# Values by seven block products of half size, 512 columns a pass

## The chip, the core and the metric

One core of a Trainium2 chip runs the whole program. Five engines work from queues of their own, in order: TensorE (PE, matmuls), VectorE (DVE), ScalarE (ACT), GpSimd (POOL) and SyncE (SP, which here only issues DMA transfers). They wait for each other by semaphores. Matmuls read SBUF and add into eight banks of PSUM; DVE and ACT read the banks out. ACT and POOL can issue transfers too. The metric is the device time of one execution in microseconds, as the median of the runs.

## The reference

A decoder trunk of two layers over 1024 tokens of width 1024, in float32. Layer 0 mixes tokens by pooling and has a gated FFN. Then keys and values for three attention branches are projected from the residual stream; layer 1 attends to them with its own queries and has an FFN. Each sub-layer is normalised and modulated by vectors computed from a conditioning vector `c`.

```python
kv_shift, kv_scale = jnp.split(cond @ kv_ada_w + kv_ada_b, 2, axis=-1)
hkv = _modulate(_rmsnorm(x, kv_norm_g), kv_shift, kv_scale)
kv = (hkv @ w_kv).reshape(b, s, 2, N_BRANCHES, N_HEADS, HEAD_DIM)
y = _dilated_attention(h, kv, attn_w_q[j], attn_w_o[j], slopes)
```

The change concerns the value half of `hkv @ w_kv`: (1024 tokens x 1024) times (1024 x 3072).

## The kernel before, in words

**Three passes for a product.** Float32 operands are split in a high part (`hi`, rounded by ACT) and a remainder (`lo`, by DVE). A product of two 128-row blocks is three matmul passes: hi x hi, hi x lo, lo x hi. `wprep` and `split` (L105 to L114) make the parts of a weight block of 128x1024; `wraw`, `whi` and `wlo` have 3, 5 and 5 buffers.

**Seven products in place of eight.** The FFN's up projection and the queries already use a seven-product scheme (class `Pair`, L404): a 2x2 block product is formed from sums of weight blocks (`s1` to `s4`, on DVE) and sums of activation blocks (`T1` to `T4`, class `Ops`), with results added in the banks pX and pY. There the weights are the stationary operand and 512 token columns move. A query pair has 7 products of 12 passes, or 5 where two were done ahead (pairs 0 to 7 of 12).

**Values, L985 to L1018.** Normalised and modulated activations (`hx`, `hkx`, then `h` in `hk`) are the stationary operand; weights move, 256 columns a pass. 12 column groups of 256, 2 token halves, 4 blocks of 128 tokens, 8 blocks of the inner dimension, 3 passes each. ACT reads a bank (`vt`) and stores 512 KB at a time to `vd` in DRAM.

**Conditioning vectors beside it, L316 to L332.** `ada_run` computes vectors 8 to 11 in the value stage: a row block `araw` of 128x1024 is loaded by SP, multiplied by the broadcast `condr` on POOL and summed in four pieces on ACT. Vectors 8 to 10 are needed at the attention's output projection and the norm after it, 11 at the second FFN's down projection.

**What sets the order.** Outside of blocks marked `manual_schedule` a scheduler with a timing model puts every engine's instructions in an order and gives tiles their buffers. The query and value stages were such code. Within a marked block the named engines follow the order in which the code was written. Attention follows, with PE in written order: key projections (from `hk`, line L1108) fill the gaps, and slabs of q and v are loaded two units ahead.

The small buffers of the query stage are the tag `t2` (5 of 128x512): the two intermediate results `qh` of a pair, the saved results `p` and `qc` that are loaded back for pairs 0 to 7.

## Time and profile before

| | us |
|---|---|
| median of 3 runs (2821.94 to 2826.0) | 2823.73 |
| the profiled execution | 2824.13 |
| its span, first to last instruction | 2822.4 |
| PE busy | 2712.8 (96%) |
| DVE busy | 1795.5 (64%) |
| ACT busy | 1197.4 (42%) |
| POOL busy | 552.8 (20%) |

The query stage ends at about 1200 us, value passes run from 1190.3 to 1474.9 us, key passes from there to 1990 us. A matmul's printed duration covers its way through the array, in which others run beside it: the cost of one in a stream is the stretch divided by the count.

### The profile page before, as it was taken

How to read it: one execution, taken by the hardware profiler on the slowest of the kernel's cores; microseconds unless marked ns; L12 is line 12 of the kernel's file. 1: busy time of each engine (PE TensorE's matmuls, PEld its weight loads, DVE VectorE, ACT ScalarE, POOL GpSimd, SP SyncE). 2: the span in 40 equal slices, each digit the busy share in tenths (PEclk: the TensorE clock that was granted, in tenths of full speed). 3: DMA queues.
4: the chain of work that ended last, by engine and by line, in shares of the span. 5: the costliest groups of instructions: out<-in, count | busy, mean ns of one | idle time of the engine just before them, and what ended most of it. 6: DMA issues, size and time to landing. Idle time of an engine off the chain costs nothing.

```text
span 2822.4 us, 38016 instructions
## 1 busy us (share of the span) xinstructions
PE 2712.8 (96%) x14220; PEld 2233.7 (79%) x14220; DVE 1795.5 (64%) x3215; ACT 1197.4 (42%) x2599; POOL 552.8 (20%) x454
## 2 busy tenths in 40 slices
PE   8988999999999999999999999999889999999997
PEld 4767888888778788899997777777667888888886
DVE  6897898776755687521114555656758986666554
ACT  4534545545541433334425444445345444443112
POOL 2476001102540300014410222222152000000001
PEclk9998999999999999999999999999999999999998
DMA  7424443334743355355532333334334432226221
GB/s 293 165 91 162 161 160 127 108 94 152 281 171 97 127 201 193 126 190 188 190 130 69 99 100 100 107 100 145 111 98 157 141 118 88 75 90 216 90 75 60
DMA packets 148825, 384.29 MB, mean 136 GB/s; under 512 B 15536, under 2 KB 53408, under 8 KB 148640
## 3 DMA queue, kind: packets, MB, share of 16 engines
q1 hardware_dynamic: 109872, 292.90, 31.2%
q10 hardware_dynamic: 26496, 50.34, 4.8%
q0 software_dynamic: 12272, 38.62, 4.2%
q8 instruction: 112, 1.84, 0.3%
q14 instruction: 73, 0.60, 0.1%
HBM read 295.75 MB, written 86.05 MB: 135 GB/s over the span
## 4 chain that ended last, share of the span: by engine, by line
PE 70%; DVE 8%; DMA 8%; issue 5%; POOL 2%; ACT 2%; SPq 0%; ACTq 0%; DVEq 0%; POOLq 0%
PE pX L414 8%; PE pX L415 8%; PE pX L416 8%; PE dps L340 5%; PE dps L341 5%; PE dps L342 5%; PE pY L414 3%; PE pY L416 3%; PE pY L415 3%; PE vps L1014 3%; PE vps L1013 3%; PE vps L1012 3%; PE kps L340 2%; DMA araw<-in_ada_t_dram 2%; PE kps L342 2%
## 5 line engine op out<-in xcount | busy, mean ns | idle before, releaser
L107 DVE TENSOR_TENSOR wlo<-wraw,whi 128x1024 fp32r<-128x1024 f32 x164 | 229.8, 1409 | 306.9 <-ACT whi L106 304.2
L340 PE MATMUL dps<-slab,whi 128*128 128x512 f32 x832 | 329.9, 398 | 12.1 <-DVE x L376 8.2
L341 PE MATMUL dps<-slab,whi 128*128 128x512 f32 x832 | 327.5, 394 | 1.1 <-DVE slab L107 1.1
L342 PE MATMUL dps<-slab,wlo 128*128 128x512 f32 x832 | 324.3, 393 | 3.5 <-DVE wlo L107 3.5
L323 POOL TENSOR_TENSOR araw<-araw,condr 128x1024 f32<-128x1024 f32 x72 | 184.7, 2570 | 601.8 <-ACT condr L894 277.2
L106 ACT ACTIVATE whi<-wraw 128x1024 fp32r<-128x1024 f32 x164 | 170.1, 1053 | 281.8 <-PE dps L341 144.5
L376 DVE SCALAR_TENSOR_TENSOR x<-dps,mods,x 128x512 f32<-128x512 f32 x280 | 202.3, 745 | 136.4 <-PE dps L342 133.7
L1185 ACT ACTIVATE ss<-ss,ngm 128x128 f32<-128x128 f32 (+1 forms) x384 | 168.0, 439 | 196.8 <-DVE ngm L1182 183.7
L1013 PE MATMUL vps<-wlo,h 128*128 128x256 f32 x768 | 217.0, 283 | 0.0
L1012 PE MATMUL vps<-whi,h 128*128 128x256 f32 x768 | 217.0, 283 | 0.0
L1014 PE MATMUL vps<-whi,h 128*128 128x256 f32 x768 | 216.3, 283 | 0.0
L340 PEld LDWEIGHTS dps<-slab,whi 128*128 128x128 f32 x832 | 158.7, 191 | 51.6 <-DVE x L376 12.4
L342 PEld LDWEIGHTS dps<-slab,wlo 128*128 128x128 f32 x832 | 158.3, 190 | 37.6 <-DVE wlo L107 4.4
L341 PEld LDWEIGHTS dps<-slab,whi 128*128 128x128 f32 x832 | 158.6, 191 | 34.0 <-DVE slab L107 1.5
L415 PE MATMUL pX<-ht,whi 128*128 128x512 f32 x448 | 174.4, 389 | 0.0
L414 PE MATMUL pX<-ht,whi 128*128 128x512 f32 x448 | 174.4, 389 | 0.0
L106 ACT ACTIVATE whi<-s 128x1024 fp32r<-128x1024 f32 x112 | 118.3, 1059 | 131.6 <-PE pY L415 78.4
L416 PE MATMUL pX<-ht,wlo 128*128 128x512 f32 x448 | 173.8, 389 | 0.0
L340 PE MATMUL kps<-h,whi 128*128 128x512 f32 x384 | 166.2, 433 | 0.0
L326 ACT ACTIVATE araw<-araw 128x256 f32<-128x256 f32 x288 | 116.4, 405 | 113.2 <-POOL araw L323 110.8
L342 PE MATMUL kps<-h,wlo 128*128 128x512 f32 x384 | 152.3, 397 | 0.0
L1178 DVE CUSTOM_DVE_ANT_0 ss<-sc,bias 128x128 f32<-128x128 f32 (+1 forms) x384 | 111.2, 345 | 64.6 <-PE sc L1172 64.3
(259 smaller groups left out, 6616.4 us busy)
## 6 DMA issues: line engine op xcount, KB each, us to landing
wraw<-in_wup_dram SPq DMA_DIRECT2D x104, 512.0 KB, 3.7
araw<-in_ada_t_dram SPq DMA_DIRECT2D x72, 512.0 KB, 4.4
gd<-at POOLq DMA_DIRECT2D x44, 512.0 KB, 3.7
wraw<-gd SPq DMA_DIRECT2D x44, 512.0 KB, 3.5
wraw<-in_wdn_dram SPq DMA_DIRECT2D x44, 512.0 KB, 4.0
wraw<-in_wq_dram SPq DMA_DIRECT2D x32, 512.0 KB, 4.2
xd<-x ACTq DMA_DIRECT2D x48, 256.0 KB, 2.0
ed<-ah ACTq DMA_DIRECT2D x24, 512.0 KB, 2.9
```

Of the source, the lines that this page charges most:

```text
L106: nc.scalar.activation(hi, raw, AF.Copy)
L107: nc.vector.tensor_tensor(lo, raw, hi.bitcast(F32), op=ALU.subtract)
L340: nc.tensor.matmul(ps, whi, hhi, start=first, stop=False)
L341: nc.tensor.matmul(ps, whi, hlo, start=False, stop=False)
L342: nc.tensor.matmul(ps, wlo, hhi, start=False, stop=last)
L376: nc.vector.scalar_tensor_tensor(xs(x, m, c), ps, g[:, m:m + 1], xs(x, m, c), op0=ALU.mult, op1=ALU.add)
L414: nc.tensor.matmul(ps, w[0][:, k], hh, start=start and j == 0, stop=False, **kw)
L415: nc.tensor.matmul(ps, w[0][:, k], hl, start=False, stop=False, **kw)
L416: nc.tensor.matmul(ps, w[1][:, k], hh, start=False, stop=j == 3, **kw)
L1012: nc.tensor.matmul(o, a, whi[:, k], start=kt == 0, stop=False)
L1013: nc.tensor.matmul(o, a, wlo[:, k], start=False, stop=False)
L1014: nc.tensor.matmul(o, b, whi[:, k], start=False, stop=kt == KT - 1)
```

## The change

- **Values.** `values` computes them in 3 column groups of 1024. In each the 1024 inner and 1024 columns of weights are a 2x2 of 512-blocks, and the tokens two halves; seven products of 4 token blocks x 4 inner blocks x 3 passes are added in banks X and Y. Activations stay the stationary operand; 512 weight columns move in a pass. DVE forms weight sums S1 to S4 in place, of which S2 needs A11, A21 and A22; A22 is loaded twice. A product's weights are prepared one product ahead (`ready(n + 1)`), loads run three ahead.
- **Activations.** `kv_norm` and `kv_sums` run in query pairs 3 to 10: normalised halves go to DRAM (`hxd`), the sums T1 to T4 too (`td`). In the first five products of the value stage they are loaded one by one (`form_load`) and split. The keys later read the same parts through `HK`; the missing quarter `hb12` is formed in the last product.
- **Conditioning.** `ada_lagged` computes vectors 8 to 10 with one buffer of two row blocks, loaded by POOL; ACT's sums for one step stand one product later. Vector 11 moves to the second FFN's up stage.
- **Order.** DVE, PE, SP and ACT are in written order through the value stage; POOL is not. The pool for `s` now comes first in the temporary space.

```diff
--- before.py
+++ after.py
@@ -571,7 +571,7 @@
     def temps_u():
         st = ExitStack()
         pools = {}
-        for tag, bufs in (("t4", 3), ("t2", 5), ("s", 2), ("h5", 1), ("l5", 1)):
+        for tag, bufs in (("s", 2), ("t4", 3), ("t2", 5), ("h5", 1), ("l5", 1)):
             pools[tag] = st.enter_context(tc.tile_pool(name="tu" + tag, bufs=bufs, reuse_waits="tile"))
         class TP:
@@ -901,6 +901,32 @@
         for i in ids:
             yield from ada_dot(i, tp, condr, tag)
+    def ada_lagged(ids):
+        condr = tp.tile([128, 1024], F32, tag="t4", name="condr")
+        nc.gpsimd.dma_start(condr, cvec[0, :].partition_broadcast(128))
+        yield
+        nc.scalar.activation(condr, condr, AF.Silu)
+        for i in ids:
+            q = cp.tile([128, 8, KQ], F32, tag="q", bufs=1, name=nm("q"))
+            for m in range(0, 8, 2):
+                rw = big.tile([128, 2, 1024], F32, tag=Q[3], name=nm("araw"))
+                for k in range(2):
+                    o = D * (i - 5) + 128 * (m + k)
+                    nc.gpsimd.dma_start(rw[:, k, :], ada_t[o:o + 128, :])
+                for k in range(2):
+                    nc.gpsimd.tensor_tensor(rw[:, k, :], rw[:, k, :], condr, op=ALU.mult)
+                yield
+                w = D // KQ
+                for k in range(2):
+                    for b in range(KQ):
+                        r = rw[:, k, w * b:w * b + w]
+                        nc.scalar.activation(r, r, AF.Copy, accum_out=q[:, m + k, b:b + 1])
+            nc.vector.reduce_sum(mod(i), q, axis=mybir.AxisListType.X)
+            nc.vector.tensor_add(mod(i), mod(i), ada_bias(i))
+            if i in scales:
+                scaleg(i, scales[i])
     def ada_steps(a, n):
         for _ in range(n):
             next(a, None)
@@ -965,6 +991,211 @@
                 nc.scalar.dma_start(qd[2 * i + 1], qt[1])
         return evac
+    hxd = dp.tile([KT, 128, 512], F32, name="hxd")
+    td = {t: dp.tile([4, 128, 512], F32, name="t" + t) for t in ("T1", "T2", "T3", "T4")}
+    hb12 = []
+    def values(ops, bd):
+        B = mod(12)
+        NG = 3
...
+        def load_a(g):
+            a = [load(rawt("wraw"), g, 0, 0, jh) for jh in range(2)]
+            raws[g] = {"A11": a}
...
+        def load_b(g):
+            raws[g]["A21"] = [load(rawt(("w4", "wraw")[jh]), g, 1, 0, jh) for jh in range(2)]
+            q = big.tile([128, 2, 1024], F32, tag=Q[2], name=nm("a22"))
+            raws[g]["A22"] = [load(q[:, jh, :], g, 1, 1, jh) for jh in range(2)]
+        def sums(g):
+            r = raws[g]
+            for jh in range(2):
+                a11, a12, a21, a22 = (r[n][jh] for n in ("A11", "A12", "A21", "A22"))
+                nc.vector.tensor_add(a22, a21, a22)
+                nc.vector.tensor_sub(a21, a11, a21)
+                nc.vector.tensor_sub(a11, a22, a11)
+            r["S2"], r["S1"], r["S3"] = r["A11"], r["A22"], r["A21"]
+        def sums4(g):
+            r = raws[g]
+            for jh in range(2):
+                nc.vector.tensor_sub(r["A12"][jh], r["A12"][jh], r["S2"][jh])
+            r["S4"] = r["A12"]
...
+        FORM = ("T2", "T1", "T3", "B22", "T4")
+        def form_load(op):
+            t = big.tile([128, 4, 512], F32, tag=Q[3], name=nm("hxl"))
+            nc.sync.dma_start(t, (hxd[4:8] if op == "B22" else td[op]).rearrange("j p c -> p j c"))
+            return t
+        def form(op, t):
+            for j in range(4):
+                hi, lo = ops.g(op, 0, j), ops.g(op, 1, j)
+                if op in ("T1", "T4"):
+                    split(t[:, j, :], hi, lo)
+                else:
+                    nrm.parts(t[:, j, :], bd[:, j:j + 1] if op == "T3" else B[:, 4 + j:5 + j], hi, lo)
...
+        def product(ps, w, op, t, start, stop):
+            ts = slice(128 * t, 128 * t + 128)
+            for j in range(4):
+                hh, hl = ops.g(op, 0, j)[:, ts], ops.g(op, 1, j)[:, ts]
+                wh, wl = (w[j // 2][i][:, 512 * (j % 2):512 * (j % 2) + 512] for i in range(2))
+                kw = {"skip_group_check": True}
+                nc.tensor.matmul(ps, hh, wh, start=start and j == 0, stop=False, **kw)
+                nc.tensor.matmul(ps, hh, wl, start=False, stop=False, **kw)
+                nc.tensor.matmul(ps, hl, wh, start=False, stop=stop and j == 3, **kw)
...
+        SEQ = (("A11", "B11"), ("A12", "B21"), ("S2", "T2"), ("S1", "T1"), ("S3", "T3"), ("S4", "B22"), ("A22", "T4"))
+        todo = [(g, i) for g in range(NG) for i in range(7)]
+        ws = {}
+        def loads(n):
+            if n < len(todo):
+                g, i = todo[n]
+                f = {0: load_a, 1: load_12, 2: load_b, 6: reload}.get(i)
+                if f is not None:
+                    f(g)
+        def ready(n):
+            if n < len(todo):
+                g, i = todo[n]
+                if i == 2:
+                    sums(g)
+                ws[n] = prep(g, SEQ[i][0])
+                if i == 3:
+                    sums4(g)
+        for j in range(4):
+            ops.sums(j)
+        aw = ada_lagged((8, 9, 10))
+        loads(0)
+        fr = form_load("T2")
+        loads(1)
+        ready(0)
+        loads(2)
+        X, Y, o, u, v = {}, {}, {}, {}, {}
+        for n, (g, i) in enumerate(todo):
+            loads(n + 3)
+            ready(n + 1)
+            if n < 5:
+                form(FORM[n], fr)
+                fr = form_load(FORM[n + 1]) if n < 4 else None
+            if n == 18:
+                ada_steps(aw, 99)
+            if n == 20:
+                for j in range(4):
+                    parts_b12(raw(hxd[j]), j)
+            op = SEQ[i][1]
+            for t in range(4):
+                if i == 0:
+                    X[t] = bank("vX")
+                elif i in (1, 3):
+                    Y[t] = bank("vY")
+                x, y = X[t], Y.get(t)
+                ps = y if i in (1, 3, 5) else x
+                product(ps, ws[n], op, t, i in (0, 1, 3), True)
...
+                elif i == 4:
+                    nc.vector.tensor_tensor(v[t], x, v[t], op=ALU.add)
+                    store(v[t], g, 1, t, 1)
...
+                if 5 <= n < 18 and t == 3:
+                    ada_steps(aw, 1)
...
+    def kv_norm(j, hx):
+        for k, ft in enumerate((j, j + 4)):
+            u, t = hx[k][:, j, :], tp.tile([128, 512], F32, tag="t2", name=nm("hxt"))
+            for c, v in enumerate((u, t)):
+                nc.sync.dma_start(v, xd[1][128 * ft:128 * ft + 128, 512 * c:512 * c + 512])
+                nc.vector.scalar_tensor_tensor(v, v, mod(13)[:, ft:ft + 1], rms[c], op0=ALU.mult, op1=ALU.mult)
+            nc.scalar.dma_start(hxd[ft], t)
+    def kv_sums(j, hx):
+        t12, t22 = (tp.tile([128, 512], F32, tag="t2", name=nm("hxt")) for _ in range(2))
+        nc.sync.dma_start(t12, hxd[j])
+        nc.sync.dma_start(t22, hxd[j + 4])
+        nc.vector.tensor_sub(t22, t22, t12)
+        nc.scalar.dma_start(td["T3"][j], t22)
+        nc.vector.tensor_sub(t12, t12, hx[0][:, j, :])
+        nc.scalar.dma_start(td["T1"][j], t12)
+        t2, t4 = (tp.tile([128, 512], F32, tag="t2", name=nm("hxt")) for _ in range(2))
+        nc.vector.tensor_add(t2, t22, hx[0][:, j, :])
+        nc.scalar.dma_start(td["T2"][j], t2)
+        nc.vector.tensor_sub(t4, hx[1][:, j, :], t2)
+        nc.scalar.dma_start(td["T4"][j], t4)
...
         for i, p in enumerate(ps_):
-            if i == 9:
-                hx = big.tile([128, 4, 512], F32, tag=Q[2], name="hx0"), big.tile([128, 4, 512], F32, tag=Q[3], name="hx1")
-                for ft in range(KT):
-                    t = hx[ft // 4][:, ft % 4, :]
-                    nc.sync.dma_start(t, xd[1][128 * ft:128 * ft + 128, 0:512])
-                    nc.vector.scalar_tensor_tensor(t, t, mod(13)[:, ft:ft + 1], rms[0], op0=ALU.mult, op1=ALU.mult)
+            if i == 3:
+                hx = [big.tile([128, 4, 512], F32, tag=t, name=nm("hx")) for t in Q[2:4]]
+            if 3 <= i < 11:
+                (kv_norm, kv_sums)[(i - 3) % 2]((i - 3) // 2, hx)
             p.rest(q_out(i))
-        hk = Hid((Q[4], Q[6], Q[5], Q[7], Q[2], Q[3], Q[8], Q[9]))
+        hv = Ops(SL0["b"], SL0["t"], XT)
+        B = mod(12)
         for ft in range(KT):
-            nrm.parts(hx[ft // 4][:, ft % 4, :], mod(12)[:, ft:ft + 1], hk.g(0, 0, ft), hk.g(0, 1, ft))
+            op = ("B11", "B21")[ft // 4]
+            nrm.parts(hx[ft // 4][:, ft % 4, :], B[:, ft:ft + 1], hv.g(op, 0, ft % 4), hv.g(op, 1, ft % 4))
+        bd = cp.tile([128, 4], F32, tag="bd", bufs=1, name=nm("bd"))
+        nc.vector.tensor_sub(bd, B[:, 4:8], B[:, 0:4])
         st0.close()
-        st0, tp = temps("tv")
-        for ft in range(KT):
-            t = tp.tile([128, 512], F32, tag="t2", name=nm("hkx"))
-            nc.sync.dma_start(t, xd[1][128 * ft:128 * ft + 128, 512:1024])
-            nc.vector.scalar_tensor_tensor(t, t, mod(13)[:, ft:ft + 1], rms[1], op0=ALU.mult, op1=ALU.mult)
-            nrm.parts(t, mod(12)[:, ft:ft + 1], hk.g(1, 0, ft), hk.g(1, 1, ft))
-
-        aw = ada_run((8, 9, 10, 11), "t4")
-        for cg in range(12):
-            if cg >= 2:
-                ada_steps(aw, 4)
-            w = [wprep(wv[cg, i]) for i in range(2)]
-            for tq in range(2):
-                vt = tp.tile([128, 4, 256], F32, tag="t4", name=nm("vt"))
...
-                    for kt in range(KT):
-                        t = slice(128 * tb, 128 * tb + 128)
-                        a, b = hk.g(tq, 0, kt)[:, t], hk.g(tq, 1, kt)[:, t]
...
-                        nc.tensor.matmul(o, a, whi[:, k], start=kt == 0, stop=False)
-                        nc.tensor.matmul(o, a, wlo[:, k], start=False, stop=False)
-                        nc.tensor.matmul(o, b, whi[:, k], start=False, stop=kt == KT - 1)
...
-                nc.scalar.dma_start(
-                    vd[512 * tq:512 * tq + 512, 256 * cg:256 * cg + 256].rearrange("(a p) c -> p a c", p=128), vt)
+        st0 = ExitStack()
+        vp = {t: st0.enter_context(tc.tile_pool(name="tv" + t, bufs=n, reuse_waits="tile"))
+              for t, n in (("w4", 3), ("t2", 9), ("t4", 1))}
+        class TV:
+            def tile(self, shape, dt, tag, name, bufs=None):
+                return vp[tag].tile(shape, dt, tag=tag, name=name)
+        tp = TV()
+        with tc.manual_schedule(engines={nc.vector.engine, nc.tensor.engine, nc.sync.engine, nc.scalar.engine}):
+            values(hv, bd)
     psU_cm.__exit__(None, None, None)
     st0.close()
     psB_cm = tc.tile_pool(name="psB2", bufs=2, space=PSUM, reuse_waits="tile")
@@ -1040,6 +1253,13 @@
         nc.gpsimd.affine_select(out=T2[:, 0:64], in_=T2[:, 0:64], pattern=[[0, 64]], compare_op=ALU.is_ge, fill=BIG,
                                 base=63, channel_multiplier=-1)
+        class HK:
+            def g(self, c, part, kt):
+                if c == 1 and kt < 4:
+                    return hb12[part][:, kt, :]
+                return hv.g((("B11", "B21"), (None, "B22"))[c][kt // 4], part, kt % 4)
+        hk = HK()
         kslab = Rows(Q[0:2], F32, "kslab")
         qslab = Rows(Q[10:12], F32, "qslab")
@@ -1341,7 +1561,8 @@
             yield
     f1 = Ffn(1, tp, hs3, SL1, xd[2], gd[1])
-    f1.up(late)
+    aw = ada_run((11,), "s")
+    f1.up(late, {i: 1 for i in range(8, 18)}, aw)
     _, late = f1.down(nrmf, done3)
     for _ in late:
         pass
@@ -1368,7 +1589,8 @@
...
-    wv = wkv[:, 3 * D:].reshape(2, 4, 128, 12, 256).transpose(3, 0, 2, 1, 4).reshape(12, 2, 128, 1024)
+    wv = np.ascontiguousarray(wkv[:, 3 * D:].reshape(2, 2, 2, 128, 3, 2, 512).transpose(4, 5, 0, 1, 3, 2, 6)).reshape(
+        3, 2, 2, 2, 128, 1024)
```

How the instructions stand. On ACT, in a middle stretch of the value stage before:

```order
L1016 ACTIVATE vt_9438<-vps_9439 128x512
L106 ACTIVATE whi_9823<-wraw_9821 128x1024
L326 ACTIVATE araw_9540,q_9302<-araw_9540 128x256 x3
L1016 ACTIVATE vt_9438<-vps_9489 128x512
L326 ACTIVATE araw_9540,q_9302<-araw_9540 128x256
L106 ACTIVATE whi_10061<-wraw_10059 128x1024
L1017 DMA vd<-vt_9438 128x4x256
L326 ACTIVATE araw_9547,q_9302<-araw_9547 128x256 x4
L1016 ACTIVATE vt_9580<-vps_9581 128x512
L326 ACTIVATE araw_9554,q_9302<-araw_9554 128x256 x4
```

and after, in the second column group (`vu`, `vv` hold results read from the banks):

```order
L924 ACTIVATE araw_9581,q_9499<-araw_9581 128x256 x8
L106 ACTIVATE whi_9673<-a_1412_9427 128x1024
L106 ACTIVATE whi_9677<-a_1412_9427 128x1024
L1157 ACTIVATE vu_9695<-vX_9513 128x512
L1157 ACTIVATE vu_9709<-vX_9528 128x512
L1157 ACTIVATE vu_9723<-vX_9543 128x512
L1157 ACTIVATE vu_9737<-vX_9558 128x512
L924 ACTIVATE araw_9668,q_9499<-araw_9668 128x256 x8
L106 ACTIVATE whi_9755<-wraw_9423 128x1024
L106 ACTIVATE whi_9759<-wraw_9425 128x1024
L1160 ACTIVATE vv_9776<-vY_9763 128x512
```

Before, the four sums of one row block stand alone between other work; after, eight sums of two blocks (`x8`) stand behind the last read of a product and ahead of the next weights (`whi`).

On POOL, which is not in written order, loads, products and the stores of L1096 now stand in one queue, and a load comes behind the products of the step before.

On DVE in the query stage, before, around the evacuations of the fourth pair (L940, L953 read banks; L454 to L460 form weight sums of a later pair):

```order
L455 TENSOR_TENSOR s_1172_7975<-s_1172_7975,wraw_7968 128x512
L940 SCALAR_TENSOR_TENSOR qt_7767<-pX_7770,qh_7823 128x512
L460 TENSOR_TENSOR s_1173_7978<-wraw_7968,s_1172_7975 128x512
L953 SCALAR_TENSOR_TENSOR qh_7909<-pX_7870,p_1152_7871 128x512
L107 TENSOR_TENSOR wlo_7980<-s_1172_7975,whi_7979 128x1024
L940 SCALAR_TENSOR_TENSOR qt_7766<-pY_7793,qh_7809 128x512
L107 TENSOR_TENSOR wlo_7986<-s_1173_7978,whi_7985 128x1024
L953 SCALAR_TENSOR_TENSOR qh_7923<-pY_7893,p_1152_7871 128x512
L940 SCALAR_TENSOR_TENSOR qt_7767<-pX_7770,p_1134_7771 128x512
L107 TENSOR_TENSOR l_1161_7890<-wraw_7873,h_1160_7889 128x512
```

and after, at the same evacuation (L966 and L979 read banks, L1189 to L1196 are the new sums of activations):

```order
L966 SCALAR_TENSOR_TENSOR qt_7786<-pX_7789,qh_7842 128x512
L1189 TENSOR_TENSOR hxt_7886<-hxt_7886,hxt_7885 128x512
L1191 TENSOR_TENSOR hxt_7885<-hxt_7885,hx_7771 128x512
L1194 TENSOR_TENSOR hxt_7893<-hxt_7886,hx_7771 128x512
L454 TENSOR_TENSOR s_1182_8020<-wraw_8018 128x512
L459 TENSOR_TENSOR s_1183_8023<-wraw_8013,wraw_8018 128x512
L455 TENSOR_TENSOR s_1182_8020<-s_1182_8020,wraw_8013 128x512
L1196 TENSOR_TENSOR hxt_7894<-hx_7772,hxt_7893 128x512
L460 TENSOR_TENSOR s_1183_8023<-wraw_8013,s_1182_8020 128x512
L966 SCALAR_TENSOR_TENSOR qt_7785<-pY_7812,qh_7828 128x512
```

Between the first evacuation and the weight sums of the later pair three new sums stand, of which the first waits for two loads of normalised blocks (`hxt`), and a fourth stands among the weight sums.

## Rows read from the trace of the kernel before

**Rows 1.** The page: busy us, share, instructions; the granted clock in 40 slices.

```profile
PE 2712.8 (96%) x14220; PEld 2233.7 (79%) x14220; DVE 1795.5 (64%) x3215; ACT 1197.4 (42%) x2599; POOL 552.8 (20%) x454
...
PEclk9998999999999999999999999999999999999998
```

**Rows 2.** Busy time by stretch: length, then busy us (count) of each engine.

```profile
core 0: us, PE busy (x) PEld busy (x) DVE busy (x) ACT busy (x) POOL busy (x), PEclk, DMA share, GB/s
1000.00:1186.00 186.00, 186.00 (x820) 153.53 (x819) 127.18 (x162) 66.03 (x84) 0.00 (x0) 1.00 0.49 170
1186.00:1215.00 29.00, 29.00 (x194) 26.79 (x193) 21.54 (x29) 10.93 (x16) 0.00 (x0) 1.00 0.81 287
1215.00:1475.00 260.00, 260.00 (x2169) 260.00 (x2168) 40.08 (x34) 104.61 (x327) 80.91 (x38) 1.00 0.49 163
```

**Rows 3.** Groups of ScalarE, 1215 to 1475: busy us, mean ns; idle before.

```profile
L326 ACT ACTIVATE araw<-araw 128x256 f32<-128x256 f32 x128 | 51.7, 405 | 45.5 <-POOL araw L323 45.2 <-DVE mods L330 0.2
L1016 ACT ACTIVATE vt<-vps 128x512 f32<-128x512 f32 x45 | 26.5, 589 | 70.1 <-PE vps L1014 62.8 <-DMA vd<-vt 7.2
L106 ACT ACTIVATE whi<-wraw 128x1024 fp32r<-128x1024 f32 x23 | 24.2, 1054 | 39.2 <-PE vps L1014 39.2
```

**Rows 4.** Groups of VectorE in a part of the query stage, 1004 to 1086.

```profile
L107 DVE TENSOR_TENSOR wlo<-s,whi 128x1024 fp32r<-128x1024 f32 x12 | 14.7, 1224 | 1.0 <-ACT whi L106 1.0
L983 DVE SCALAR_TENSOR_TENSOR hx<-hx,mods,rs 128x512 f32<-128x512 f32 x8 | 5.6, 756 | 0.0
...
L454 DVE TENSOR_TENSOR s<-wraw 128x512 f32<-128x512 f32 x6 | 4.1, 690 | 10.3 <-DMA wraw<-in_wq_dram 10.3
```

**Rows 5.** Waits of ScalarE, 1215 to 1475: us in total, times, longest.

```profile
ACT araw L326 <- POOL araw L323: 45.2, 21, 6.0
```

**Rows 6.** Timeline of SP, POOL, ACT, 1307 to 1320: start us, us.

```profile
1308.71 1.02 SPq L322 DMA_DIRECT2D araw<-in_ada_t_dram  x2
...
1312.93 5.75 POOL L323 TENSOR_TENSOR araw<-araw,condr 128x1024 f32<-128x1024 f32 x2 [8.46 <-DMA araw<-in_ada_t_dram]
...
1318.71 0.42 ACT L326 ACTIVATE araw<-araw 128x256 f32<-128x256 f32 x1 [0.20 <-POOL araw L323]
```

**Rows 7.** Line 532: issue of a 512 KB store by POOL, ns min/median/max.

```profile
L532 POOL DMA_DIRECT2D gd<-at x44: 531/533/756, 356.1 to 2563.8; - x44
```

**Rows 8.** Lines 323 and 322 in 1215 to 1475: ns min/median/max; DMA landing.

```profile
L323 POOL TENSOR_TENSOR araw<-araw,condr x32: 2393/2402/3395, 1242.5 to 1426.9; 128x1024 f32<-128x1024 f32 x32
...
DMA to landing us min/median/max: 3.3/4.8/8.4
```

**Rows 9.** Busy time in the stretch of about one query pair.

```profile
1058.00:1072.00 14.00, 14.00 (x63) 11.32 (x62) 10.14 (x15) 5.78 (x6) 0.00 (x0) 1.00 0.46 157
```

**Rows 10.** Waits of SP and VectorE, 1000 to 1186.

```profile
SPq L445 <- DVE qt L940: 21.8, 4, 10.1
SPq L947 <- DVE qt L940: 11.5, 6, 2.2
...
DVE s L454 <- DMA wraw<-in_wq_dram: 20.0, 8, 4.0
```

**Rows 11.** DMA issues: count, KB each, median us from issue to landing.

```profile
xd<-x ACTq DMA_DIRECT2D x48, 256.0 KB, 2.0
...
qslab<-qd SPq DMA_DIRECT2D x24, 512.0 KB, 3.2
...
hx<-xd SPq DMA_DIRECT2D x8, 256.0 KB, 4.4
```

**Rows 12.** Busy time in the two FFNs' up stages.

```profile
270.00:600.00 330.00, 326.67 (x1446) 269.57 (x1445) 276.92 (x372) 165.94 (x278) 40.86 (x30) 1.00 0.40 134
2170.00:2560.00 390.00, 389.56 (x1718) 322.08 (x1718) 291.39 (x399) 173.40 (x230) 11.26 (x21) 1.00 0.33 114
```

**Rows 13.** Group of VectorE, 1215 to 1475.

```profile
L107 DVE TENSOR_TENSOR wlo<-wraw,whi 128x1024 fp32r<-128x1024 f32 x23 | 38.2, 1662 | 216.8 <-ACT whi L106 216.8
```

60 lines of the change are left out of this document (52 added, 8 removed).

## The prediction

> **What bounds the kernel now.** I read the page's busy shares first: TensorE (PE) is busy 96% of the span and the clock row shows 9 nearly throughout, the second of the two levels (2.4 GHz) [rows 1]. So time can be won in two ways only: fewer or cheaper PE passes, or less PE idle time. Then I cut the span into stretches [rows 2]. In the last part of the query stage (1000 to 1186 us), in the 29 us where queries and values overlap, and in the rest of the value stage (1215 to 1475 us) PE is busy 100% at granted clock 1.00, while VectorE (DVE) is at 68%, 74% and 15%. No engine makes PE wait there. What is taken off PE in the value stage comes off the time, unless something new makes PE wait.
>
> The same rows give the price of a pass, as stretch over count. Matmuls are pipelined, so the duration printed for one (283 ns for 256 columns) is not its cost. 260.0 us / 2169 = 0.1199 us for a pass of 256 columns; 186.0 / 820 = 0.2268 us for one of 512 [rows 2]. At 2.4 GHz the columns alone take 0.1067 and 0.2133 us, so either pass carries about 13 ns beside its columns.
>
> **The PE part of the change.** Before: 12 column groups x 2 token halves x 4 token blocks x 8 k-blocks x 3 = 2304 passes of 256 columns. After: 3 groups x 7 products x 4 token blocks x 4 k-blocks x 3 = 1008 passes of 512. That is 7/8 of the columns in 7/16 of the passes. Moving 512 columns past a 128x128 stationary block is what the query passes already do, so I price the new pass by them. 2304 x 0.1199 = 276.2 us; 1008 x 0.2268 = 228.6 us. PE saves **47.6 us**: 30.7 us by columns (73,728 at 2.4 GHz), 17 us by 1296 fewer fixed costs of 13 ns.
>
> The Trainium skill, "TensorE: Matmul & The Clock Gate", section "Back-to-back issue gap", gives a lone pass N/2.4 + 2.5 ns. By that the saving would be an estimated 33.9 us and the total some 14 us higher. The rows here show 13 ns beside the columns, not 2.5, and they decide.
>
> **The other engines in the new value stage.** One product is 48 passes, 48 x 0.2268 = 10.9 us. In that time ScalarE (ACT) makes two high halves of weights (1.05 us each), evacuates up to four banks (0.59 each) and, in 12 of the 21 products, does eight summing passes of the conditioning (0.404 each) [rows 3]: 2.1 + 2.4 + 3.2 = 7.7 us. DVE makes two low halves (1.22 each) and at most six weight sums of the same size or four bank additions of about 0.7 [rows 4], below 10 us. On busy time both fit. What can cost is order: all queues but GpSimd's (POOL's) now stand in the written order.
>
> *The conditioning loop.* Before, its rows went through four buffers, loaded by SP; ACT sat 45.2 us in this stretch waiting for POOL's products, at no cost, since PE was busy throughout [rows 2, 5]. After, one buffer of two halves is used over and over: POOL issues two loads, multiplies two halves, ACT sums them, and only then may POOL load again. ACT's eight sums stand ahead of the weights of the product after next. So the loop has a period of its own, and where it is above 10.9 us ACT falls behind. A pair of loads in the trace: issued at 1308.71, the second product done at 1312.93 + 5.75 = 1318.68, so 9.97 us, and ACT starts at 1318.71 [rows 6]. Four sums after that are 1.62: period 11.6 us. POOL's own issue is 0.53 us a transfer [rows 7]; the store issues that fall between the two products lie in the gap in which the second load is still landing (5.75 less 2 x 2.40 = 0.95 us [rows 6, 8]). Twelve steps have 11 intervals: 11 x (11.6 - 10.9) = 7.8 us of lag. From it goes the slack: 10.9 less a last evacuation 0.6, sums 3.2, weights 2.1 and the low half 1.2 leaves 3.8. I take **+4 us**. Bounds: with the shortest landing, 3.3, the period is 0.5 + 3.3 + 4.8 + 1.6 = 10.2 and the cost zero; with the longest landing, 8.4, and the longest product, 3.40, twice [rows 8], it is 0.5 + 8.4 + 6.8 + 1.6 = 17.3, which is 11 x 6.4 - 3.8 = 67 us.
>
> *The start.* Value passes still begin inside the last query pair. But in the 17 us of the first one and a half products the second product's weights, four more half-blocks for the sums (4 x 0.5 MB) and the first formed operand (1 MB) must land, then six sums and two low halves run on DVE one after another (8 x 1.13 to 1.22 = 9.5 us). At the 287 GB/s of the overlap before [rows 2] 4 MB take 14 us. I take **+2 us**; bounds 0 and 8.
>
> *The query stage.* Four pairs get four products with the norm (DVE 0.75 each), four get four sums (0.69) [rows 4], together 32 DVE instructions where 8 were in this stage: 2.4 to 2.7 us more per pair of 13.6 us (60 passes). A pair's stretch before has DVE at 10.14 of 14 us [rows 9], so about 90% after. Also new are 16 more loads on SP (24 for 8) and 24 stores on ACT's queue, all through the five small buffers that the evacuations use, and a load that waits for a buffer holds up the weight loads queued behind it on SP. Before, SP already waited there 33.3 us for such buffers and DVE 20.0 us for weights, in waits up to 4.0 us, and PE never [rows 2, 10]. Lower bound 0 by that. Upper bound: each of the four summing pairs comes late by a load (4.4), three sums and a store (2.0) [rows 4, 11], 8.2 us, 33 us in all. The scheduler has put the next pair's first two products ahead of the evacuation that could be late, so I stay near the lower end: **+4 us**.
>
> *The end.* The first query slabs for attention now take the buffers of operands that the last product still reads; before, they went out while the first values were computed. PE has 72 key passes (16 us) before the first scores, against 3.2 us for a slab [rows 11]. Slabs, values and key weights together are some 4 MB in those 16 us. **+2 us**, 0 to 10.
>
> *The twelfth conditioning vector* moves to the second FFN's up stage. The first FFN carries the same loop there, and PE shows no loss that could be put down to it: 326.7 busy of 330 (its start is in that stretch), 389.6 of 390 in the second without it [rows 12]. I count 0, at most 3; cover is PE's 19 us a pair.
>
> **Sum.** 2824.1 (the profiled execution) - 47.6 + 4 + 2 + 4 + 2 = 2788.5; this execution lies 0.4 above the median of the runs, so **2788 us**.
>
> **Rivals.**
> 1. *No wait at all.* For it: PE waited for nothing in 475 us around the change [rows 2]. Against it: the pair of loads gives 11.6, not 10.9. 2824.1 - 47.6 - 0.4 = 2776 us.
> 2. *DVE and POOL block each other.* The low halves on DVE take 1.66 us in the value stage, where POOL multiplies, and 1.22 in the query stage, where POOL is idle [rows 2, 4, 13]; POOL's product takes 2.40, at most 3.40 [rows 8]. If every product takes the longer time, the period is 11.6 + 2 x 1.0 = 13.6, the loss 11 x 2.7 - 3.8 = 26 in place of 4: 2810 us. Against it: in the loop's beat the low halves come right after the sums, while POOL's next load is under way. The Trainium skill, "SBUF — State Buffer", section "Who interferes with whom", states the rule: a DVE tensor_tensor with both inputs in SBUF and a GpSimd instruction that reads SBUF exclude each other for a whole instruction. The two durations of the low half agree with it.
> 3. *The query stage pays in full*: +33 in place of +4 gives 2817 us. For it: SP's waits and five buffers. Against: the order has work in hand.
> 4. *The loop sets the pace, and the kernel gets slower.* ACT, in order, holds weights back behind the sums of a loop whose loads land late in the fuller DMA (163 GB/s before [rows 2]; the stage gets 3 MB more of weights and 6 MB of operands, 4 MB less of conditioning rows, and is shorter). At 8.4 us a landing and 3.40 a product the loss is 67: 2788 + 63 = 2851 us. It decides from a period at which 11 x (P - 10.9) - 3.8 + 8 = 47.6, P = 14.9 us; the pair in the trace speaks against it.
>
> **Chances.** Forecast (waits of 5 to 25 us in all) 0.58; no wait 0.13; DVE against POOL 0.10; query stage 0.08; slower loop 0.06; some other sum of waits that leaves about nothing 0.05. A measurement of this kernel can tell about 0.2%, 5.6 us, from no change. Faster: 0.58 + 0.13 + 0.09 + 0.06 = 0.86. Same: 0.01 + 0.02 + 0.04 = 0.07. Slower: 0.06 + 0.01 = 0.07. The likeliest case by itself spans 2779 to 2800; 2773 to 2818 takes in no wait, both partial rivals and little beyond.
>
> **What would show it.** Right: the new value passes at 0.227 us each, the stage some 235 us from its first to its last pass; in its middle third ACT waiting for POOL's product before each block of sums, a period of 11 to 12 us, and PE waiting for a high or low half in single waits of 1 to 2 us from about the tenth product of the loop on; PE busy above 97% of the query stage. Wrong: passes well off 0.227, PE idle by more than 10 us in the query pairs 3 to 10 behind the small buffers, a loop period of 13 us or more, or a wait for query slabs at the first scores.

## The result and the profile after

The changed kernel took **2790.14 us** (median of 4 runs, 2784.17 to 2792.55) against 2823.99, a ratio of 0.9877 with a 95% interval of 0.986 to 0.9894. The forecast was 2788, the range 2773 to 2818. Measured again on another chip it took 2798.11 us against 2825.63, ratio 0.9906 (0.989 to 0.9922): in the range too, and 10 us above the forecast. Which terms the two results hold is the subject of what follows.

The page of the profiled execution after the change, its engines and the granted clock (answers to [rows 1]):

```profile
PE 2666.8 (96%) x12924; PEld 2145.4 (77%) x12924; DVE 1891.0 (68%) x3326; ACT 1219.6 (44%) x2634; POOL 605.0 (22%) x527
...
PEclk9998999999999999999999999999999999999998
```

PE has 46.0 us less to do and its share stays 96%; the span became 34.1 us shorter (2822.4 to 2788.3 us). By stretch (length, busy us of PE, PEld, DVE, ACT, POOL with counts, clock, DMA share, GB/s; answers to [rows 2]): the query pairs, the value stage, and four of its products:

```profile
1000.00:1186.00 186.00, 181.10 (x782) 147.85 (x781) 138.63 (x182) 58.73 (x73) 0.00 (x0) 0.98 0.63 218
1215.00:1440.00 225.00, 213.17 (x930) 174.99 (x929) 120.41 (x128) 114.46 (x295) 99.70 (x92) 0.98 0.52 189
1324.19:1367.79 43.60, 43.60 (x194) 35.96 (x192) 12.68 (x17) 23.35 (x77) 29.63 (x28) 1.00 0.61 223
```

The four products are 192 passes in 43.60 us, 0.2271 us each (the row's 194 counts two that reach in from before): the new pass costs what a query pass costs, as forecast. But PE is no longer busy throughout: 4.9 us idle in the queries and 11.8 in the value stage, each with a clock of 0.98 where 1.00 stood. PE's longest waits from 975 to 1460 us (in all, times, longest):

```profile
PE vX L1091 <- DVE wlo L107: 8.6, 2, 7.2
PE pX L414 <- ACT whi L106: 3.4, 1, 3.4
PE vX L1090 <- ACT whi L106: 2.8, 1, 2.8
PE pY L414 <- DVE qh L979: 1.5, 1, 1.5
```

Five waits hold 16.3 us. Their full price is more, since some of them are followed by passes at the lower clock. In what follows a loss is how much later PE's passes start than 0.2268 us after the one ahead, summed over a group; it holds the wait and the slow passes behind it. For the queries the sum goes over all passes that start from 1000 to 1186 us: it is 9.0 us here, where the kernel before has 0.4. The expectations of the later runs, printed below, count only the largest group there.

**The large stall, 1379 to 1393 us.** This is in front of the third column group's S2 product. PE by slices of 4 us (columns as above):

```profile
1378.00:1382.00 4.00, 1.56 (x7) 0.94 (x6) 3.97 (x5) 0.77 (x1) 1.51 (x3) 1.00 0.69 259
1382.00:1386.00 4.00, 0.50 (x1) 0.19 (x1) 3.93 (x3) 0.29 (x1) 4.00 (x2) 0.64 0.01 3
1386.00:1390.00 4.00, 0.00 (x0) 0.00 (x0) 4.00 (x2) 1.07 (x2) 1.82 (x1) 0.50 0.00 0
1390.00:1394.00 4.00, 3.91 (x11) 3.11 (x12) 3.64 (x6) 4.00 (x17) 1.40 (x3) 0.58 0.18 66
```

PE stands for 7 us between its first and its second pass, and where it works again the clock is 0.50 to 0.58 before it is 1.00: seven passes follow each other at 0.43 us, the lower of the two levels, before the pitch is 0.2268 again. The loss of the group is 12.0 us, and 12.7 with a short wait of a low half just ahead of it, at 1368. What led to it, from the chain of waits that ends there (start, us, what):

```profile
1366.92 3.64 DMA araw<-in_ada_t_dram
...
1370.63 4.75 POOL araw L918 x2
...
1375.41 1.72 ACT araw L924 x8
...
1377.15 0.20 DVE mods L925
...
1377.46 1.22 DVE a L1032
...
1388.82 1.22 DVE wlo L107
...
1390.09 0.79 PE vX L1091
```

Read from the top: the load of a pair of conditioning rows, POOL's two products, ACT's eight sums, then DVE's *reduction* of the finished vector (L925), and only behind it the six weight sums for S2. Two of these sums take 3.25 us, not 1.22, and POOL's next two products run beside them, from 1381.32 to 1387.8 (start, us):

```profile
1382.37 3.25 DVE L1033 TENSOR_TENSOR wraw<-wraw,wraw 128x1024 f32<-128x1024 f32 x1
1385.65 3.25 DVE L1034 TENSOR_TENSOR wraw<-a,wraw 128x1024 f32<-128x1024 f32 x1
```

```profile
1381.32 6.50 POOL L918 TENSOR_TENSOR araw<-araw,condr 128x1024 f32<-128x1024 f32 x2 [2.49 <-DMA araw<-in_ada_t_dram]
```

The group rows of DVE in the value stage show long instructions too (busy us, mean ns; [rows 13] answers the first):

```profile
L107 DVE TENSOR_TENSOR wlo<-wraw,whi 128x1024 fp32r<-128x1024 f32 x30 | 39.3, 1339 | 55.1 <-ACT whi L106 55.0
...
L1033 DVE TENSOR_TENSOR wraw<-wraw,wraw 128x1024 f32<-128x1024 f32 x6 | 9.4, 1562 | 0.2
```

**The loop's period.** ACT's first sum of a pair of rows stands 11.9, 12.2 and 11.4 us after the one before (the first is 1337.62). Over the seven intervals of the loop up to the stall the mean is 11.5 us, in the repeat below 11.9; single ones go from 10.5 to 13.1. POOL's product is as in [rows 8]:

```profile
1349.49 0.42 ACT L924 ACTIVATE araw<-araw 128x256 f32<-128x256 f32 x1 [4.75 <-POOL araw L918]
...
1361.68 0.42 ACT L924 ACTIVATE araw<-araw 128x256 f32<-128x256 f32 x1 [3.14 <-POOL araw L918]
...
1373.05 0.42 ACT L924 ACTIVATE araw<-araw 128x256 f32<-128x256 f32 x1 [2.87 <-POOL araw L918]
```

```profile
L918 POOL TENSOR_TENSOR araw<-araw,condr x24: 2382/2400/3387, 1283.9 to 1424.1; 128x1024 f32<-128x1024 f32 x24
```

**The queries.** The large wait there is at 1080. SP, ACT and DVE ahead of it (start, us):

```profile
1067.72 0.32 SPq L973 DMA_DIRECT2D qc<-ed  x1
...
1074.97 0.33 SPq L102 DMA_DIRECT2D wraw<-in_wq_dram  x1
...
1072.65 1.14 ACT L974 ACTIVATE qt<-qc 128x512 f32<-128x512 f32 x1 [3.18 <-DMA qc<-ed]
...
1073.58 0.64 ACT L106 ACTIVATE h<-wraw 128x512 fp32r<-128x512 f32 x1
...
1082.75 1.06 ACT L106 ACTIVATE whi<-s 128x1024 fp32r<-128x1024 f32 x1 [8.54 <-DVE s L455]
...
1074.25 0.69 DVE L107 TENSOR_TENSOR l<-wraw,h 128x512 fp32r<-128x512 f32 x1 [1.89 <-ACT h L106]
...
1079.02 1.41 DVE L1181 SCALAR_TENSOR_TENSOR hxt<-hxt,mods,rs 128x512 f32<-128x512 f32 x2 [3.48 <-DMA hxt<-xd]
1080.83 0.69 DVE L454 TENSOR_TENSOR s<-wraw 128x512 f32<-128x512 f32 x1 [0.40 <-DMA wraw<-in_wq_dram]
```

A load of a saved result (`qc`, issued at 1067.72 after a wait for one of the five small buffers) lands at 1072.65; ACT's copy of it stands ahead of the high half `h`, this ahead of DVE's `l`, which frees the weights' buffer; the next weights go out at 1074.97 and land at 1080.8. The norm of a new block waits in front of their sum on DVE too, but no longer than the weights do. So in this trace the weights are issued late, behind the small buffers, and then take 5.8 us to land, where the median of these loads is 4.9. The DMA share of 1000 to 1186 is 0.63 where it was 0.49.

### The profile page after: what moved, and what is told of

The parts are those of the page before. It is cut to its first block, busy times and chain, and to the rows that moved or that the text cites. A ratio compares the mean times of both kernels' runs of the same rounds, so it can differ in the third digit from the quotient of the medians.

```text
span 2788.3 us, 35767 instructions
## 1 busy us (share of the span) xinstructions
PE 2666.8 (96%) x12924; PEld 2145.4 (77%) x12924; DVE 1891.0 (68%) x3326; ACT 1219.6 (44%) x2634; POOL 605.0 (22%) x527
## 4 chain that ended last, share of the span: by engine, by line
PE 36%; DVE 5%; DMA 4%; issue 4%; POOL 1%; ACT 1%; SPq 0%; DVEq 0%; ACTq 0%; POOLq 0%
PE dps L340 3%; PE dps L342 3%; PE dps L341 3%; PE pX L414 3%; PE pX L415 3%; PE pX L416 3%; PE kps L340 2%; PE kps L341 2%; PE kps L342 2%; PE pY L414 1%; PE pY L415 1%; PE pY L416 1%; PE sc L1392 1%; PE pv L1427 1%; DVE ss L1398 1%
## 5 line engine op out<-in xcount | busy, mean ns | idle before, releaser
L340 PE MATMUL dps<-slab,whi 128*128 128x512 f32 x832 | 328.7, 396 | 12.2 <-DVE x L376 6.8
L106 ACT ACTIVATE whi<-wraw 128x1024 fp32r<-128x1024 f32 x172 | 177.2, 1051 | 251.2 <-PE dps L341 143.6
L323 POOL TENSOR_TENSOR araw<-araw,condr 128x1024 f32<-128x1024 f32 x48 | 132.5, 2767 | 322.7 <-DMA araw<-in_ada_t_dram 289.6
L341 PEld LDWEIGHTS dps<-slab,whi 128*128 128x128 f32 x832 | 158.2, 190 | 33.9 <-DVE slab L107 1.1
L340 PE MATMUL kps<-hb,whi 128*128 128x512 f32 x384 | 165.4, 431 | 0.7 <-ACT vw L1169 0.7
L342 PE MATMUL kps<-hb,wlo 128*128 128x512 f32 x384 | 151.8, 395 | 0.0
L341 PE MATMUL kps<-hb,whi 128*128 128x512 f32 x384 | 151.6, 395 | 0.0
L107 DVE TENSOR_TENSOR wlo<-s,whi 128x1024 fp32r<-128x1024 f32 x112 | 138.6, 1240 | 7.7 <-ACT whi L106 7.2
L414 PE MATMUL pX<-hb,whi 128*128 128x512 f32 x320 | 127.9, 403 | 11.7 <-ACT ah L432 10.1
L503 DVE SCALAR_TENSOR_TENSOR at<-at,P 128x512 f32<-128x512 f32 (+2 forms) x176 | 134.8, 771 | 5.6 <-ACT at L500 4.9
```

Source lines behind the costliest of these rows:

```text
L106: nc.scalar.activation(hi, raw, AF.Copy)
L107: nc.vector.tensor_tensor(lo, raw, hi.bitcast(F32), op=ALU.subtract)
L340: nc.tensor.matmul(ps, whi, hhi, start=first, stop=False)
L341: nc.tensor.matmul(ps, whi, hlo, start=False, stop=False)
L342: nc.tensor.matmul(ps, wlo, hhi, start=False, stop=last)
L414: nc.tensor.matmul(ps, w[0][:, k], hh, start=start and j == 0, stop=False, **kw)
```

## The experiments

**The changed kernel again.** No edit.

> The changed kernel once more, so that the variants have their own base on the same chip. All theories: 2784 to 2793 us, ratio to before near 0.988. What the repeat decides: in the first profile PE lost 11.9 us at 1379 to 1393 (in front of the product with S2 of the third column group) and about 8 us in the query pairs, while attention was 4.6 us shorter and the stretch up to the queries 4.3 us shorter than before. If these two gains are the change's, they stand again within 1 us; if they are the scatter of one execution, they come out different by 2 us or more.

2798.11 us, six runs from 2791.91 to 2804.37: above the range that was expected. PE's longest waits in the same stretch:

```profile
PE vX L1091 <- DVE wlo L107: 8.2, 3, 7.2
PE pX L414 <- ACT whi L106: 3.6, 1, 3.6
PE vX L1090 <- ACT whi L106: 3.3, 2, 3.1
```

The losses are about the same at the same places: queries 8.2 (9.0 in the first profile), ahead of the third S2 product 13.9 and 1.5 just before (12.7). The gains elsewhere are not: from the first score to the last `pv` pass it was 554.9 us before, 550.4 in the first profile and 555.6 here; the norm ahead of the queries came 4.3 us earlier in the first profile, 1.8 later here. The ten profiles of the changed kernel and its variants, whose code is the same in both places, go from 549.2 to 555.6 us for the one and from 975.0 to 981.3 for the other (979.5 before). So some 9 us of the first result are the scatter of single executions in stretches that the change does not touch.

**The reduction one product later.**

```diff
                 yield
+                reduce()        # of the vector finished one product ago
                 ...             # ACT's sums
-            nc.vector.reduce_sum(mod(i), q, axis=mybir.AxisListType.X)
-            nc.vector.tensor_add(mod(i), mod(i), ada_bias(i))
+            done.append((i, q))
```

> The reduction of a conditioning vector (DVE) stands one product later, behind the weight sums and low halves; nothing is left out. Theory 1 (DVE's queue: the reduction waits for ACT's eight sums, and the sums for S2 and the low halves queue behind it): the stall of 10.3 us ahead of the third S2 product falls to 0 to 4 us, since the sums can start 7 us earlier but may still meet POOL's products; total 5 to 11 us less than the changed kernel, 2779 to 2785. Theory 2 (the loop's own period makes ACT late, my prediction's reason): ACT's sums and high halves come as before, so the stall stays within 2 us and the time within 2 us of the changed kernel. Theory 3 (POOL's products alone stretch DVE's six sums from 1.23 to 3.25): they do so wherever the sums meet products; gain 0 to 4 us.

2791.33 us, ratio 0.988 (0.9865 to 0.9895): 7 us under the changed kernel on that chip, as theory 1 expected; its total of 2779 to 2785 was missed, since that kernel itself took 2798 there. The stall ahead of the third S2 product fell to 2.8 us. DVE's sums for S2 now start at 1368.78, where they started at 1377.46 (1.9 us of this because the whole value stage stands earlier in this profile), and show theory 3 by itself:

```profile
1368.78 1.22 DVE L1040 TENSOR_TENSOR a<-wraw,a 128x1024 f32<-128x1024 f32 x1
1370.03 3.47 DVE L1041 TENSOR_TENSOR wraw<-wraw,wraw 128x1024 f32<-128x1024 f32 x1
1373.53 3.30 DVE L1042 TENSOR_TENSOR wraw<-a,wraw 128x1024 f32<-128x1024 f32 x1
1376.76 1.21 DVE L1040 TENSOR_TENSOR a<-wraw,a 128x1024 f32<-128x1024 f32 x1
```

The two sums beside POOL's products take 3.47 and 3.30 us, the others 1.21 to 1.23. So the reduction made the sums late, and POOL makes them long. Waits of low halves remained, since the loop and POOL are as before:

```profile
PE vX L1099 <- DVE wlo L107: 6.5, 5, 2.7
```

One of them repeats the cause at another place. The third vector's reduction has no later product to move to and still stands right behind ACT's sums. DVE stands idle for 7.78 us until these are there, four bank additions and the low half of the last product come behind it, and PE loses 3.7 us at 1426. The changed kernel lost nothing at that product: after its larger stall ACT's sums began 10.9 us ahead of it, here 6.0.

```profile
1424.08 0.19 DVE L914 TENSOR_REDUCE mods<-q 128x8 f32<-128x32 f32 x1 [7.78 <-ACT araw L934]
```

**POOL's multiplication left out.**

```diff
-                for k in range(2):
-                    nc.gpsimd.tensor_tensor(rw[:, k, :], rw[:, k, :], condr, op=ALU.mult)
```

> POOL's multiplication of the conditioning rows in the value stage is left out (ACT sums the rows as loaded; the result is another one). Theory 1: ACT's sums end 4.8 us sooner and so does the reduction; the stall ahead of the third S2 product falls from 10.3 to 0 to 3 us. Theory 2 (period of the loop): the period falls from 11.6 to 6.8, all of the stall goes. Theory 3 (POOL stretches DVE): low halves in the value stage 1.22 us everywhere, no sum of 3.25, stall 3 to 6 us since the reduction still waits. Total 2777 to 2785 for 1 and 3, 2777 to 2779 for 2.

2785.11 us, 13 under the changed kernel; the loss ahead of S2 was 1.9 us, the only one over 1 us in the value stage. DVE's groups there:

```profile
L107 DVE TENSOR_TENSOR wlo<-wraw,whi 128x1024 fp32r<-128x1024 f32 x32 | 38.0, 1222 | 66.4 <-ACT whi L106 66.4
...
L1031 DVE TENSOR_TENSOR wraw<-wraw,wraw 128x1024 f32<-128x1024 f32 x6 | 7.4, 1225 | 0.2
```

Every low half takes 1.22 us and every sum 1.23. This is theory 3 as far as durations go; the loss of 1.9 us is theory 1's 0 to 3, not theory 3's 3 to 6. Since the loop no longer falls behind either (ACT's sums stand 10.8 us apart in the mean, not the 6.8 of theory 2, and a product takes 10.9), this run alone does not tell the loop from the stretched sums.

**The product on DVE**, the reduction late as above.

```diff
-                    nc.gpsimd.tensor_tensor(rw[:, k, :], rw[:, k, :], condr, op=ALU.mult)
                 yield
+                    nc.vector.tensor_tensor(rw[:, k, :], rw[:, k, :], condr, op=ALU.mult)
                 ...             # ACT's sums
```

> The multiplication moves from POOL to DVE, one product after the load, and the reduction is one product later as in the run before; nothing is left out. DVE gets 24 x 1.23 = 29 us more work in a stage where it was busy 120 of 225 us. Theories 1 and 3 together: no reduction in front of the weight sums and no POOL instruction beside them, so the stall goes whole, 10 to 12 us less than the changed kernel: 2776 to 2781. Theory 2: ACT's sums now wait for DVE's products, which stand behind four additions of a product; ACT is late by up to 2.5 us a product and the time is within 3 us of the changed kernel or above it.

2778.37 us, ratio 0.9836 (0.9818 to 0.9855), and on another chip, as base for the last two runs:

> The version with the product on DVE once more, as the base on this chip for the two others: 2774 to 2784 us, one loss of 4 to 5 us at 1081 in the query pairs and none over 1 us in the value stage. Were the loss in the queries scatter, it would stand at another place or be missing.

2781.29 us, 0.9842 (0.9826 to 0.9858). PE's longest waits from 975 to 1445 in the first of the two:

```profile
PE pX L414 <- ACT whi L106: 2.7, 1, 2.7
PE kps L340 <- ACT vw L1177: 0.7, 1, 0.7
```

The value stage has none left, with 28.6 us more work on DVE. From the norm ahead of the queries (979.5 us before, 976.65 and 975.23 here) to the last value pass it is 453.5 and 454.1 us where it was 495.4: 41.9 and 41.3 less, which with the losses of 6.4 and 7.0 us in the queries (0.4 before) is the 47.6 of PE's passes within 0.5. Theory 2's version of this run (ACT late behind DVE) did not come.

**Passes of 256 columns.** Every value pass cut in two (on the version above). The two halves of a bank are started one by one, so its values are not the sums that they should be; passes, columns and operands are.

```diff
+            for c in (slice(0, 256), slice(256, 512)):
                 for j in range(4):
                     ...
-                    nc.tensor.matmul(ps, hh, wh, ...)
+                    nc.tensor.matmul(ps[:, c], hh, wh[:, c], ...)
```

> The version with the product on DVE, with every value pass cut in two of 256 columns (2016 passes in place of 1008; same columns, same operands, nothing left out). If a pass carries about 13 ns beside its columns, as the two pitches of the kernel before gave (0.1199 and 0.2268 us), value passes take 2016 x 0.1199 = 241.7 in place of 228.6 us and the kernel is 13 us slower than the version with the product on DVE: about 2791. If the width of a pass were nothing and only the seven products counted, the time would stay within 3 us of 2778; if PE cannot hide the load of the stationary block behind 256 columns, it would be 20 us or more slower.

2797.52 us, 0.9894 (0.9872 to 0.9915), 16 to 19 above its base, where 13 were expected; in the profile the same stretch is 14.5 us longer.

```profile
1230.00:1340.00 110.00, 110.00 (x919) 110.00 (x919) 64.55 (x70) 54.32 (x122) 16.36 (x31) 1.00 0.54 195
```

918 to 919 passes in 110 us, 0.1197 to 0.1198 us: the pitch of the kernel before. So the width of the passes is worth some 13 to 15 us of the 47.6, and the seven products the rest.

**Own places for the activations' blocks.** Norms and sums of the query stage in quarters of `hx` that are still empty (on the version with the product on DVE).

```diff
-            u, t = hx[k][:, j, :], tp.tile([128, 512], F32, tag="t2", ...)
+            u, t = hx[k][:, j, :], hx[k][:, j + 1, :]        # j < 3
...
-        nc.sync.dma_start(t12, hxd[j])
-        nc.sync.dma_start(t22, hxd[j + 4])
```

> The version with the product on DVE, in which the activations' norms and sums of the query stage use the not yet filled quarters of hx in place of the five small buffers (but for the last block of each), and the sums find their operands there in place of loading them again; nothing is left out. Theory 1 (small buffers: stores of the sums hold them, so the loads of saved results come late, then the saved copy on ACT, the high half behind it, the release of the weights' buffer and so the next weights): the loss of 4.4 to 6.3 us that stands at 1061 to 1081 in all four runs goes to under 1.5, total 3 to 6 us less than 2778. Theory 2 (the transfers are slow because the DMA engines are busier, 0.6 to 0.8 in these pairs): six fewer loads of 256 KB out of 48 new transfers change little, loss 3 us or more at a place in the query pairs. Theory 3 (DVE is full): the count of DVE instructions stays, so the loss stays.

2775.48 us, 0.9821 (0.98 to 0.9841). What theory 1 expected did not come: the loss at 1080 went, but one of 5.3 us came at 1061 (6.1 in all in the queries, where the version with the product on DVE has 6.4 and 7.0). There:

```profile
1040.00:1050.00 10.00, 10.00 (x44) 7.94 (x43) 6.24 (x11) 1.36 (x3) 0.00 (x0) 1.00 0.92 331
1050.00:1060.00 10.00, 10.00 (x45) 8.12 (x44) 9.50 (x15) 3.39 (x4) 0.00 (x0) 1.00 0.93 302
1060.00:1070.00 10.00, 6.53 (x23) 4.91 (x22) 7.59 (x11) 2.12 (x2) 0.00 (x0) 0.83 1.01 356
```

The DMA engines are busy 0.92 to 1.01 for 30 us, at up to 356 GB/s. Weights issued at 1053.65 land at 1061.98, after 8.3 us, where the median of these loads is 4.8; the sum on DVE that waits for them starts at 1062.07, and the bank read (`qh`) that PE waits for stands behind it. This is another wait than the one at 1080 of the changed kernel, where the weights were issued late and landed in 5.8 us.

**Three of four stores of the sums left out** (on that version).

```diff
-        nc.scalar.dma_start(td["T1"][j], t12)
-        nc.scalar.dma_start(td["T2"][j], t2)
-        nc.scalar.dma_start(td["T4"][j], t4)
```

> The run with the spare quarters of hx, in which three of four stores of the activations' sums (T1, T2, T4: 12 of 16, 3 MB) are left out; the value stage reads T3 in their place, so loads and passes stay and only values differ. There PE lost 5.0 us at 1061, behind weights that landed late while the DMA engines were 0.92 to 1.01 busy from 1040 to 1070. Theory 2 (bursts of transfers delay the weights): the share of 1040 to 1070 falls to about 0.85 and the loss to under 1.5 us; total 2771 to 2776. Theory 3 (DVE full) or an order that is late in any case: the loss stays at 3 to 6 us, since no instruction of DVE is left out.

2775.0 us, 0.9818 (0.9802 to 0.9835), which the time of the run before does not differ from; the loss in the queries is 3.1 us.

```profile
1040.00:1050.00 10.00, 10.00 (x45) 8.03 (x43) 8.54 (x14) 1.42 (x3) 0.00 (x0) 1.00 0.96 332
1050.00:1060.00 10.00, 8.53 (x37) 6.68 (x36) 8.36 (x12) 3.01 (x4) 0.00 (x0) 1.00 0.94 311
1060.00:1070.00 10.00, 9.68 (x43) 8.03 (x44) 9.03 (x14) 3.63 (x4) 0.00 (x0) 1.00 0.82 282
```

The loss fell by half with no DVE instruction gone, which speaks for the transfers and against DVE; but the share fell from 1060 on only, so the number that I expected of it was wrong, and a part of the loss stayed. The stores also held the quarters that they read (SP waited 23.7 us for them in the run before, here 12.7 for DVE's sums), so an earlier issue is not told apart from a faster landing.

**Norms and sums in the last four pairs** (on the version with the product on DVE).

```diff
-            if 3 <= i < 11:
-                (kv_norm, kv_sums)[(i - 3) % 2]((i - 3) // 2, hx)
+            if 8 <= i < 12:
+                kv(i - 8, hx)        # norm and sums of one block, sums in place
```

> The version with the product on DVE, in which the activations' norms and sums stand in query pairs 8 to 11 (norm and sums of one block in one pair, the sums on the normalised blocks in place, so that 8 loads go); nothing is left out. Pairs 8 to 11 load no saved results and last 19 us, not 13.6, with the same weights. Theory 2 (bursts of transfers): no loss in the queries, as before the change; total 2771 to 2775. Theory 3 (DVE full): 8 to 10 more DVE instructions in each of four pairs, 5.5 to 7 us of 19, make a loss there of 3 us or more. Against both: T2 is stored late, and the first value products could wait for it, up to 5 us at the start of the value stage.

PE in the queries, and DVE's 142.35 us where the base has 139.94:

```profile
1000.00:1186.00 186.00, 184.80 (x812) 151.66 (x811) 142.35 (x189) 62.68 (x79) 0.00 (x0) 1.00 0.61 209
```

The losses in the queries are 2.3 us where the base has 7.0. In the last four pairs, where theory 3 expected 3 us or more, 1.1 us were lost, at 1146, with DVE busy 0.77 of 1120 to 1186. That speaks against theory 3 but does not settle it: from 1040 to 1070, ahead of the base's loss, DVE's work fell too (25.05 to 18.52 us), together with the DMA share (0.76 to 0.62). The third value product, the first that takes T2, waits 2.0 us for a low half; up to 5 were feared. The time is 2780.74 us, 0.9841 (0.9826 to 0.9855), over the 2771 to 2775 that theory 2 gave and no better than its base on that chip (2781.29): a gain of 2 to 4 us can't be told in the times of executions that scatter by 9.

The four runs with the product on DVE that compute the whole (0.9821 to 0.9842) beat both results of the changed kernel: their intervals end at 0.9858 or lower, where the changed kernel's first begins at 0.986 and its second at 0.989. Among themselves they overlap.

## Why the prediction was right, and where it was not

- **PE's saving, 47.6: right.** The pitch is 0.2271 by the row of four products, and in the two runs with the product on DVE the stretch up to the last value pass is 41.9 and 41.3 us shorter with 6.4 and 7.0 lost in the queries. The Trainium skill's gap for a lone pass ("TensorE: Matmul & The Clock Gate", section "Back-to-back issue gap", 2.5 ns beside the columns) would have made it an estimated 33.9; the pitches after the change agree with the 13 ns of the rows before, not with it.
- **The conditioning loop, +4: mechanism half right, size wrong (12.7; 15.4 in the repeat).** The period of 11.6 was right in the mean (11.5; 11.9 in the repeat), and the first wait of a low half (0.4 us, at 1368) came about where I had put it. The step that failed is "11 x (11.6 - 10.9) = 7.8 us of lag. From it goes the slack". It counted ACT's queue alone. The end of a vector puts a reduction into DVE's queue that waits for ACT's sums, and at the second vector the six weight sums of the next S2 are the first thing behind it. With the reduction moved the stall was 2.8 us, and where the third vector's reduction could not move, PE lost 3.7. That the period itself came out is part luck. I had read the 0.95 us by which the pair of products in [rows 6] exceeds 2 x 2.40 as the landing of the second load. The trace before has that load landed at 1314.38, while the first product still ran; the second product took 3.39 us, beside a low half of 2.83:

```profile
1313.58 2.83 DVE L107 TENSOR_TENSOR wlo<-wraw,whi 128x1024 fp32r<-128x1024 f32 x1 [18.78 <-ACT whi L106]
```

```profile
L323 POOL TENSOR_TENSOR araw<-araw,condr x2: 2400/2894/3387, 1312.9 to 1315.3; 128x1024 f32<-128x1024 f32 x2
```

So the pair was one of rival 2. Without it the same sum gives 10.6 us, under a product's 10.9, and a cost of nothing.
- **Rival 2, DVE against POOL, was given 0.10 and took part.** Against it I had said that the low halves come "right after the sums, while POOL's next load is under way". Two low halves met products all the same (2.59 and 3.41 us, at 1284.82 and 1287.33) and cost PE nothing. What cost was the weight sums for S2, which stand where POOL multiplies: 3.25 to 3.47 us for 1.23. The rule of the Trainium skill ("SBUF — State Buffer", section "Who interferes with whom"), that a DVE tensor_tensor with both inputs in SBUF and a GpSimd instruction that reads SBUF keep each other out for a whole instruction, agrees: the sums that met no product took 1.21 to 1.23, and without the product all did.
- **The clock was in no term.** After the wait of 3.4 us in the queries 12 passes came 0.43 us after the one ahead of them (2.4 us more in all), after the one of 7.3 in the value stage six; after a wait of 1.4 us none did. The length of a wait alone does not tell: with the reduction moved, none followed the stall of 2.8 us at 1379 and seven followed the shorter wait of 1.9 at 1426. So a wait was often worth more than its length.
- **The start, +2: right** (1.6, and under 1 in the repeat). **The end, +2:** 17.6 us from the last value pass to the first score where 16.6 stood, so 1.0. **The twelfth vector, 0: right;** the second up stage after the change is busy 380.00 of 380 us (2130 to 2510).
- **The query stage, +4: 9.0 and 8.2.** The place was right (weights behind the small buffers' loads). The upper bound's mechanism, a summing pair late by a load of its own, was not seen (and its terms add up to 4.4 + 3 x 0.69 + 2.0 = 8.5 us, not 8.2). In the changed kernel's own trace the small buffers make the weights go out late. With own places that loss went and one of the same size came behind weights that landed late among many transfers, and with three of four stores left out half of it stayed. So small buffers alone are not the reason. How buffers, transfers and order share the 9.0 us of the changed kernel is open, and that DVE's added work has no part in it is not shown.

Added up, the losses are 9.0 + 1.6 + 12.7 + 1.0 = 24.3 where I had 12. The kernel was to land near 2800 by that, as its repeat did (2798); the first result came 10 us lower by the scatter of stretches that the change leaves alone. So the forecast's hit of 2 us is part luck; its direction, its main term and its range are not.

## What to carry to other kernels

When a loop of several engines is put beside a full engine, follow not only the loop's period but its last step: an instruction that waits for the loop in a third engine's written order makes everything behind it wait, and it costs most where that engine's longest block of work comes next. Price a wait of PE with the passes that follow it at the lower clock, where the trace has any: here up to 2.4 us on a wait of 3.4. And look at what a duration met before building a period on it: the pair of products here held a collision. Repeat the changed kernel before explaining a hit: stretches that nobody touched moved by 4 us each.

## What was not expected

Two products of POOL and two sums of DVE that meet take 6.50 us on both engines, where alone they want 4.80 and 2.46. POOL's long products here, up to 3.39 us, were in the trace before as well [rows 8]; what they cost the other engine shows only in its own rows, as the 1.66 us of the low halves in [rows 13].
